# Two blocks of a modulation vector, moved from one attention stage to another

## The chip, the cores and the metric

One core of a Trainium2 chip runs the whole program in one launch. The metric is the device time of that launch in microseconds (us). Three runs of the kernel before were timed, and one more execution was recorded by the hardware profiler.

## The reference, cut to what matters

Two blocks follow each other on 512 tokens of width 1024. The first is a layer with differential attention (4 heads), neighbourhood attention (16 heads), a mixture of 32 experts and a gated per-layer term. The second has two layers, each with its own modulation vector: a grouped-query attention layer, and a latent-attention layer. What matters here is that vector, which depends on the conditions alone and on nothing that the first block computes:

```python
def adaln_params(cond, w_mod, b_mod):
    mod = jax.nn.silu(cond) @ w_mod + b_mod          # w_mod: 1024 x 3072
    return jnp.split(mod, 3, axis=-1)                # shift, scale, gate

def hybrid_layer(x, ctx, c, c_ctx, ...):
    shift, scale, gate = adaln_params(c, w_mod, b_mod)
    h = rms_norm_2(x, norm_w) * (1.0 + scale[:, None, :]) + shift[:, None, :]
    y, yc = mixer(h, hc, mixer_params, cos, sin, with_ctx_out)
    x = x + gate[:, None, :] * y
```

The gate of the second layer is thus first needed when that layer's output is added to x, at the very end of the program. Shift and scale of that layer are needed much earlier, for the context tokens too.

## The kernel before, in words

Everything is in float32, with the large products split in a high and a low part. The stages follow each other: input projections, 4 differential heads and then 4 groups of neighbourhood heads (32 steps in one loop, `run_groups(heads + ...)`, L1341), the output product of that layer, a router, 32 experts whose weights stream in from HBM, a gate, the grouped-query layer (its projections, then 8 pairs of heads of 4 steps each, L1692), its output product, and the latent layer.

**The modulation vectors** come from the generator `mod_steps` (L678). A vector of 3072 columns is computed in 6 blocks of 512 columns. Each block needs 4 transfers of 512 KB (tile `raw`, from the pool RAW), and from each of these 16 small matmuls: 128 x 32 weights (`cv`, the two conditions in a tile that is zero elsewhere) against 128 x 128 of `raw`, one in each quarter of the columns of the array, 64 in a block. DVE adds the bias (`bm`) into `ms` (L707). After 6 blocks `ms` is stored to HBM (L712). Blocks 0 and 1 are the shift, 2 and 3 the scale, 4 and 5 the gate. Four transfers are asked for ahead, one more each time one was used.

**Where its work lies.** `mod_step` (L1333) is called after each of the 32 steps of the loop of L1341 and draws the next block at every second one from step 2: layer 0 at steps 2 to 12, layer 1 at 14 to 24. So all 12 blocks lie beside the differential and neighbourhood heads. The same `mod_step` calls `late` (L1337), which asks for the first four tiles of the output weights `w_out` at step 27, into RAW too, and splits one at each of the steps 29 to 32; at step 30 it asks for the first expert's weights.

**The grouped-query loop.** `gqa_step` (L1688) is called after each of its 32 steps. It draws from `qkv` (projections of later heads, whose weights pass through RAW as well; these end early in the loop) and calls `late` (L1690), which again asks for four tiles of output weights at step 27 and splits them at steps 29 to 32. One step of `attn_pair` (L517 to L530) computes for each of two heads the scores (PE, `s<-stk`), a row maximum (DVE, L524) and the exponentials (ACT, L526) into a tile `pr`, for the second head taken from RAW:

```python
p = ((W, RAW)[h] if nk > 512 else T2)([P, nk], name="pr")
```

The tiles of two steps are transposed together two steps later (`turn_two`, L550), and until then they hold their slots. RAW has 4 slots (`N_RAW`, L36). All loads and stores are issued by one queue, SP, in order (L128). The framework places the instructions on the engines by the order of the program and a simulated time; a tile waits for a free slot of its pool.

Of the kernel before, what the change touches and what calls it, by code (L numbers as in the profile page):

```python
# [17 lines left out]
OP = mybir.AluOpType  # L18
# [4 lines left out]
P = 128  # L23
# [17 lines left out]

PREP_LEAD = 2
D_PRE, GQA_PRE, MLA_PRE = 5, 14, 34
MOD_FROM, EARLY = 2, 30
CTX_FROM, CTX_RATE, CTX_FINE = 2, 1.65, 3
PREL, OVF_AT, PLE_AT, PLE_FIRST = 2, 24, 29, 2
MLA_ST, MLA_FIRST, MLA_MIX = 2, 8, (1, 3)
# [35 lines left out]
def block_kernel(ctx: ExitStack, tc: tile.TileContext, I, out, dbg=None):  # L83
    nc = tc.nc
# [12 lines left out]
    def allocator(p):  # L97
        def f(shape, dt=F32, name=p):
            return pool[p].tile(shape, dt, name=name, tag=p)
        return f  # L100

    XT, RAW, W, Y, K3, T2 = (allocator(p) for p in pool)
# [10 lines left out]
    def D1(dt=F32):  # L113
        return psD.tile([P, 512], dt, name="d1", tag="d1")
# [13 lines left out]
    def load(dst, src):  # L128
        nc.sync.dma_start(dst, src)

    store = load
# [371 lines left out]
    mod_d = [dr.tile([2, 3 * D], F32, name=f"mod{i}") for i in range(2)]  # L503
# [171 lines left out]
        nc.vector.tensor_tensor(y, y, Bs, op=OP.add)  # L675
        return make_X(y, 8)

    def mod_steps(cv):  # L678

        wv = [I[f"l{l}_w_mod_2"].rearrange("(p c) n -> p c n", c=8) for l in range(2)]

        def ask(n):
            t = RAW([P, 2, 512], name="raw")
            load(t, wv[n // 24][:, n % 4 * 2:n % 4 * 2 + 2, n // 4 % 6 * 512:(n // 4 % 6 + 1) * 512])
            return t

        ring = [ask(n) for n in range(4)]
        yield  # L690
        for l in range(2):
            bm = Y([P, 8, P], name="bm")
            nc.vector.memset(bm, 0.0)
            for i in range(2):
                load(bm[i::32], I[f"bm{l}"])
            ms = Y([P, 6, P], name="ms")
            for b in range(6):
                ps = D1()
                for j in range(4):
                    raw = ring.pop(0)  # L700
                    for k in (2 * j, 2 * j + 1):
                        for g in range(4):
                            mm(ps[32 * g:32 * g + 32, :P], cv[:, k], raw[:, k % 2, g * P:(g + 1) * P], k == 0, k == 7)
                    n = 24 * l + 4 * b + j + 4
                    if n < 48:
                        ring.append(ask(n))
                nc.vector.tensor_tensor(ms[:, b], ps[:, :P], bm[:, b], op=OP.add)  # L707
                if b < 5:
                    yield
            nc.vector.scalar_tensor_tensor(ms[:, 2:4], ms[:, 2:4], 1.0, bm[:, 6:8], op0=OP.add, op1=OP.mult)  # L710
            for i in range(2):
                store(mod_d[l][i].rearrange("(b g n) -> g b n", b=6, g=4), ms[i::32])  # L712
            yield

    def rope_rows(name, gains, go, tab, d, scale=1.0):
# [378 lines left out]
    for j, off in enumerate((31, 23, 15)):  # L1094
        load(raw_d[j].rearrange("c h d k -> (h d) c k"), ap_of(I["rpb"], off, [[64, 240], [-1, 16], [1, 32]]))
        t = Y([P, 30, 32], name="btab")
# [102 lines left out]
        pass  # L1199


    cv = T2([P, 8, 32], name="cv")
    c2 = SM([P, 2, 8], "c2", bufs=1)
    cth = SM([P, 2, 8], "cth", bufs=1)
    load(c2, I["c2s"])
    nc.vector.memset(cv, 0.0)
    nc.scalar.activation(cth, c2, AF.Tanh, scale=0.5)
    nc.vector.scalar_tensor_tensor(cth, cth, 1.0, c2, op0=OP.add, op1=OP.mult)
    nc.vector.tensor_scalar(cv[:, :, 0:2], cth.rearrange("p i k -> p k i"), 0.5, None, op0=OP.mult)


    def nbr_group(g):
# [91 lines left out]
        return prep, 4, (A, turn, values), end, LAG_N  # L1304

    beside[0] = False
    fill, units = mod_steps(cv), [0]
    next(fill)
    w_out_v = I["w_out"].rearrange("(c p) n -> p c n", p=P)
    b_out = [Dense(w_out_v, 8, [(b * 512, 512)], OT, place=() if b else [Y] * 6) for b in range(2)]  # L1310
# [236 lines left out]
    _, wts, yidx, oidx, ovf_e, novf = res  # L1547
# [137 lines left out]
    pairs[0] = prepared(pairs[0], qkv, GQA_PRE)  # L1685
    late = split_late(b_out[0], 32)

    def gqa_step():  # L1688
        next(qkv, None)
        late()  # L1690

    run_groups(pairs, gqa_step)  # L1692
    beside[0] = False

    def residual(l, src, bs, fin, nxt=()):

# [118 lines left out]
    todo = list(chain(*grp))  # L1815
# [148 lines left out]
```

## Time and profile before

| what | us |
|---|---|
| three runs of the kernel before, median | 1866.92 |
| lowest and highest of the three | 1862.93, 1869.68 |
| the profiled execution, its device time | 1867.22 |
| span in that profile, first to last instruction | 1865.4 |
| PE busy, share of the span | 1669.5, 89% |
| DVE busy | 968.3, 52% |
| ACT busy | 743.6, 40% |
| POOL busy | 441.3, 24% |

The profile's engines are PE (matmuls), PEld (its weight loads, beside PE), DVE, ACT, POOL and SP (the queue of transfers). The device time is 1.8 us longer than the span. PE is the busiest engine over the whole span, but a share of the span is a mean over stages that have different limits, so each stage is read by itself.

### The profile page before, as it was taken

Reading aid. Unit: us, or ns where it says so; the run is one execution under the profiler, and the core shown is the slowest. Engines: PE = TensorE matmul, PEld = TensorE weight load, DVE = VectorE, ACT = ScalarE, POOL = GpSimd, SP = SyncE. Lnnn points to the kernel's source line nnn. Section 1 sums busy time; section 2 is a strip of 40 time slices with the busy share of each in tenths; the row PEclk is TensorE's granted clock in tenths of the full one; section 3 lists DMA queues with packets and bytes.
Section 4 is the critical chain, followed back from the end, with each engine's and each line's share of the span. In section 5 each row is a group of like instructions: output and inputs, shape, how many; then the busy total and the mean of one; then the engine's idle time right before and its main releaser. Section 6 shows DMA issues by size and latency. Waiting matters only on the chain. (4 is left out here: it accounts for less than half of the span.)

```text
span 1865.4 us, 28201 instructions
## 1 busy us (share of the span) xinstructions
PE 1669.5 (89%) x10297; PEld 1191.7 (64%) x10297; DVE 968.3 (52%) x2237; ACT 743.6 (40%) x1623; POOL 441.3 (24%) x590
## 2 busy tenths in 40 slices
PE   7998878969999989899897799999989889779988
PEld 6887656756555545455553588766657878656757
DVE  6865567343323131311323876666653657886752
ACT  5344557212222222221212443356661534656750
POOL 0531221002221202123101312232111424333221
PEclk9999978979999999999897899999989989999999
DMA  9456667598999999988999452100032435332041
GB/s 253 153 184 221 222 197 226 191 349 312 393 406 402 317 405 335 382 302 307 375 389 376 146 171 90 35 1 1 1 130 96 142 109 165 112 100 63 23 136 46
DMA packets 189983, 385.33 MB, mean 207 GB/s; under 512 B 28184, under 2 KB 86136, under 8 KB 189840
## 3 DMA queue, kind: packets, MB, share of 16 engines
q1 hardware_dynamic: 186384, 375.08, 56.7%
q0 software_dynamic: 3456, 8.39, 1.3%
q8 instruction: 83, 1.36, 0.3%
q14 instruction: 60, 0.49, 0.1%
HBM read 348.86 MB, written 38.13 MB: 207 GB/s over the span
## 5 line engine op out<-in xcount | busy, mean ns | idle before, releaser
L150 PE MATMUL d<-we,exT 128*64 128x256 f32 x2048 | 254.8, 392 | 12.8 <-DMA we<-in_w 8.9
L150 PE MATMUL d<-whi,Xhi 128*128 128x512 f32 (+2 forms) x560 | 219.4, 392 | 3.8 <-ACT Xhi L390 1.5
L150 PE MATMUL d<-whi,Xlo 128*128 128x512 f32 (+2 forms) x560 | 218.1, 390 | 5.2 <-DVE Xlo L182 5.2
L150 PE MATMUL d<-wlo,Xhi 128*128 128x512 f32 (+2 forms) x560 | 217.3, 388 | 0.0
L150 PEld LDWEIGHTS d<-we,exT 128*64 128x64 f32 x2048 | 146.6, 140 | 103.9 <-issue 24.7
L242 ACT CAST whi<-raw 128x1024 fp32r<-128x1024 f32 (+2 forms) x130 | 131.4, 1019 | 134.1 <-PE d L150 80.1
L524 DVE TENSOR_REDUCE ast<-s 128x1 f32<-128x768 f32 (+1 forms) x160 | 135.0, 848 | 77.0 <-PE s L150 75.0
L526 ACT ACTIVATE pr<-s,ast 128x768 f32<-128x768 f32 (+1 forms) x160 | 131.2, 821 | 58.9 <-DVE ast L524 54.6
L153 PE MATMUL t<-ident,pr 128*128 128x128 f32 x832 | 125.8, 280 | 16.4 <-ACT PT L179 9.3
L150 PE MATMUL s<-stk 128*128 128x256 f32 x448 | 121.8, 357 | 20.6 <-ACT pr L526 15.4
L251 DVE TENSOR_TENSOR wlo<-raw,whi 128x1024 fp32r<-128x1024 f32 (+2 forms) x88 | 107.7, 1234 | 40.9 <-ACT whi L242 23.7
L150 PE MATMUL d<-we,eth 128*64 128x512 f32 x512 | 121.8, 608 | 5.3 <-DVE eth L1441 5.3
L150 PEld LDWEIGHTS d<-whi,Xhi 128*128 128x128 f32 x560 | 107.6, 192 | 27.6 <-ACT Xhi L390 3.0
L153 PEld LDWEIGHTS t<-ident,pr 128*128 128x128 f32 x832 | 96.1, 142 | 45.0 <-ACT PT L179 14.2
L248 POOL TENSOR_TENSOR wlo<-raw,whi 128x512 fp32r<-128x512 f32 (+2 forms) x69 | 82.2, 1220 | 178.0 <-ACT whi L242 77.3
L150 PEld LDWEIGHTS d<-whi,Xlo 128*128 128x128 f32 x560 | 107.4, 192 | 26.3 <-DVE Xlo L182 6.7
L150 PE MATMUL d<-whi,ot 128*128 128x512 f32 x384 | 120.1, 392 | 1.9 <-DVE rT L1298 1.3
L150 PEld LDWEIGHTS d<-wlo,Xhi 128*128 128x128 f32 x560 | 107.7, 192 | 19.7 <-DVE wlo L251 0.3
L1433 DVE SCALAR_TENSOR_TENSOR eth<-eth,d 128x256 f32<-128x256 f32 x32 | 13.5, 421 | 156.3 <-ACT eth L1432 152.2
L150 PEld LDWEIGHTS s<-stk 128*128 128x128 f32 x448 | 71.0, 196 | 36.8 <-ACT pr L526 22.5
L150 PEld LDWEIGHTS d<-whi,ot 128*128 128x128 f32 x384 | 71.9, 188 | 19.1 <-issue 1.8
L150 PE MATMUL s<-whi,Xhi 128*128 128x512 f32 (+2 forms) x192 | 75.1, 395 | 9.0 <-ACT pr L526 7.2
(470 smaller groups left out, 3034.3 us busy)
## 6 DMA issues: line engine op xcount, KB each, us to landing
we<-in_w SPq DMA_DIRECT2D x378, 512.0 KB
raw<-in_l_w_mod SPq DMA_DIRECT2D x48, 512.0 KB
raw<-in_l_w_in SPq DMA_DIRECT2D x64, 256.0 KB
raw<-in_w_in SPq DMA_DIRECT2D x24, 512.0 KB
raw<-in_l_w_out SPq DMA_DIRECT2D x24, 512.0 KB
raw<-in_l_w_in SPq DMA_DIRECT2D x16, 512.0 KB
y_d<-ey SPq DMA_DIRECT2D x64, 128.0 KB
bias<-bias SPq DMA_DIRECT2D x48, 128.0 KB
```

The source lines that it names most:

```text
L150: nc.tensor.matmul(o, l, r, start=start, stop=stop)
L153: nc.tensor.transpose(o, x, identr if x.dtype == F32R else ident)
L242: nc.scalar.copy(t, src)
L248: e.tensor_tensor(t, src[:, k], hi[k].bitcast(F32), op=OP.subtract)
L251: e.tensor_tensor(t, src, whole.bitcast(F32), op=OP.subtract)
L524: nc.vector.tensor_reduce(st[:, h:h + 1], ps, op=OP.max, axis=AX.X, negate=True)
L526: nc.scalar.activation(p, ps, AF.Exp, bias=st[:, h:h + 1], accum_out=sums[:, c, h:h + 1])
L1433: nc.vector.scalar_tensor_tensor(th[:, 256:], th[:, :256], 1.0, ps[:, :256], op0=OP.add, op1=OP.mult)
```

## The change

The generator takes a list of parts (layer, first block, last block) and the conditions. In the first loop it is given layer 0 whole and blocks 0 to 3 of layer 1. A second generator with blocks 4 and 5 of layer 1 (the gate) is drawn in `gqa_step` from step 23: at step 23 it makes `cv` again and asks for four transfers, at step 24 it computes block 4, at step 25 block 5 and the stores. Each generator loads its own bias tile.

```diff
--- before.py
+++ after.py
@@ -41,7 +41,7 @@
 
 PREP_LEAD = 2
 D_PRE, GQA_PRE, MLA_PRE = 5, 14, 34
-MOD_FROM, EARLY = 2, 30
+MOD_FROM, EARLY, GATES_FROM = 2, 30, 23
 CTX_FROM, CTX_RATE, CTX_FINE = 2, 1.65, 3
 PREL, OVF_AT, PLE_AT, PLE_FIRST = 2, 24, 29, 2
 MLA_ST, MLA_FIRST, MLA_MIX = 2, 8, (1, 3)
@@ -675,41 +675,48 @@
         nc.vector.tensor_tensor(y, y, Bs, op=OP.add)
         return make_X(y, 8)
 
-    def mod_steps(cv):
+    def mod_steps(cth, parts):
 
 
 
         wv = [I[f"l{l}_w_mod_2"].rearrange("(p c) n -> p c n", c=8) for l in range(2)]
+        todo = [(l, b, j) for l, b0, b1 in parts for b in range(b0, b1) for j in range(4)]
 
         def ask(n):
+            l, b, j = todo[n]
             t = RAW([P, 2, 512], name="raw")
-            load(t, wv[n // 24][:, n % 4 * 2:n % 4 * 2 + 2, n // 4 % 6 * 512:(n // 4 % 6 + 1) * 512])
+            load(t, wv[l][:, j * 2:j * 2 + 2, b * 512:(b + 1) * 512])
             return t
 
-        ring = [ask(n) for n in range(4)]
+        cv = T2([P, 8, 32], name="cv")
+        nc.vector.memset(cv, 0.0)
+        nc.vector.tensor_scalar(cv[:, :, 0:2], cth.rearrange("p i k -> p k i"), 0.5, None, op0=OP.mult)
+        n = 4
+        ring = [ask(i) for i in range(n)]
         yield
-        for l in range(2):
+        for l, b0, b1 in parts:
             bm = Y([P, 8, P], name="bm")
             nc.vector.memset(bm, 0.0)
             for i in range(2):
                 load(bm[i::32], I[f"bm{l}"])
             ms = Y([P, 6, P], name="ms")
-            for b in range(6):
+            for b in range(b0, b1):
                 ps = D1()
                 for j in range(4):
                     raw = ring.pop(0)
                     for k in (2 * j, 2 * j + 1):
                         for g in range(4):
                             mm(ps[32 * g:32 * g + 32, :P], cv[:, k], raw[:, k % 2, g * P:(g + 1) * P], k == 0, k == 7)
-                    n = 24 * l + 4 * b + j + 4
-                    if n < 48:
+                    if n < len(todo):
                         ring.append(ask(n))
+                        n += 1
                 nc.vector.tensor_tensor(ms[:, b], ps[:, :P], bm[:, b], op=OP.add)
-                if b < 5:
+                if b < b1 - 1:
                     yield
-            nc.vector.scalar_tensor_tensor(ms[:, 2:4], ms[:, 2:4], 1.0, bm[:, 6:8], op0=OP.add, op1=OP.mult)
+            if b0 == 0:
+                nc.vector.scalar_tensor_tensor(ms[:, 2:4], ms[:, 2:4], 1.0, bm[:, 6:8], op0=OP.add, op1=OP.mult)
             for i in range(2):
-                store(mod_d[l][i].rearrange("(b g n) -> g b n", b=6, g=4), ms[i::32])
+                store(mod_d[l][i].rearrange("(b g n) -> g b n", b=6, g=4)[:, b0:b1], ms[i::32, b0:b1])
             yield
 
     def rope_rows(name, gains, go, tab, d, scale=1.0):
@@ -1199,14 +1206,11 @@
         pass
 
 
-    cv = T2([P, 8, 32], name="cv")
     c2 = SM([P, 2, 8], "c2", bufs=1)
     cth = SM([P, 2, 8], "cth", bufs=1)
     load(c2, I["c2s"])
-    nc.vector.memset(cv, 0.0)
     nc.scalar.activation(cth, c2, AF.Tanh, scale=0.5)
     nc.vector.scalar_tensor_tensor(cth, cth, 1.0, c2, op0=OP.add, op1=OP.mult)
-    nc.vector.tensor_scalar(cv[:, :, 0:2], cth.rearrange("p i k -> p k i"), 0.5, None, op0=OP.mult)
 
 
     def nbr_group(g):
@@ -1304,7 +1308,7 @@
         return prep, 4, (A, turn, values), end, LAG_N
 
     beside[0] = False
-    fill, units = mod_steps(cv), [0]
+    fill, units = mod_steps(cth, [(0, 0, 6), (1, 0, 4)]), [0]
     next(fill)
     w_out_v = I["w_out"].rearrange("(c p) n -> p c n", p=P)
     b_out = [Dense(w_out_v, 8, [(b * 512, 512)], OT, place=() if b else [Y] * 6) for b in range(2)]
@@ -1685,12 +1689,19 @@
     pairs[0] = prepared(pairs[0], qkv, GQA_PRE)
     late = split_late(b_out[0], 32)
 
+    gates, done = mod_steps(cth, [(1, 4, 6)]), [0]
+
     def gqa_step():
         next(qkv, None)
+        done[0] += 1
+        if done[0] >= GATES_FROM:
+            next(gates, None)
         late()
 
     run_groups(pairs, gqa_step)
     beside[0] = False
+    for _ in gates:
+        pass
 
     def residual(l, src, bs, fin, nxt=()):
```

## Rows read from the trace of the kernel before

**Rows 1.** page, part 2: 40 slices of 46.6 us, in tenths

```profile
PE   7998878969999989899897799999989889779988
PEclk9999978979999999999897899999989989999999
DMA  9456667598999999988999452100032435332041
```

**Rows 2.** windows: length, busy PE, PEld, DVE, ACT, POOL, clock, DMA, GB/s

```profile
250.00:270.00 20.00, 15.54 (x222) 11.26 (x211) 10.68 (x44) 10.28 (x27) 5.52 (x7) 0.83 0.91 282
270.00:290.00 20.00, 16.15 (x184) 11.93 (x185) 14.32 (x51) 13.83 (x37) 4.17 (x7) 0.82 0.71 216
290.00:310.00 20.00, 16.87 (x151) 12.16 (x152) 15.93 (x54) 15.08 (x44) 3.62 (x5) 0.84 0.57 177
```

**Rows 3.** tile cv: matmuls; windows of it (PE, PEld, DVE, clock)

```profile
L150 PE MATMUL d<-raw,cv x768: 269/273/423, 151.5 to 284.5; 128*32 128x128 f32 x192
...
257.00:267.00 10.00, 3.78 (x64) 2.18 (x64) 0.00 (x0) 0.66 1.03 326
280.00:285.00 5.00, 3.61 (x64) 2.76 (x64) 0.00 (x0) 0.72 0.61 214
150.00:290.00 140.00, 34.08 (x768) 22.70 (x768) 0.34 (x2) 0.88 0.71 226
```

**Rows 4.** timeline of PE: start, us, instruction [idle before <- releaser]

```profile
257.95 0.64 PE L150 MATMUL d<-raw,cv 128*32 128x128 f32 x16 [3.09 <-DMA raw<-in_l_w_mod]
...
259.90 1.08 PE L150 MATMUL d<-raw,cv 128*32 128x128 f32 x16 [0.19 <-DMA raw<-in_l_w_mod]
...
262.25 1.08 PE L150 MATMUL d<-raw,cv 128*32 128x128 f32 x16 [0.25 <-DMA raw<-in_l_w_mod]
```

**Rows 5.** tile nsb on ACT, 245 to 285, 285 to 335 us

```profile
L1266 ACT ACTIVATE nsb<-nsb,nst x20: 492/494/512, 252.1 to 282.5; 128x256 f32<-128x256 f32 x20
...
L1266 ACT ACTIVATE nsb<-nsb,nst x36: 488/494/511, 291.4 to 324.3; 128x256 f32<-128x256 f32 x36
```

**Rows 6.** windows of the expert stage, columns as in rows 2

```profile
500.00:600.00 100.00, 92.69 (x630) 55.73 (x630) 30.95 (x98) 24.47 (x66) 17.83 (x24) 1.00 1.03 405
700.00:800.00 100.00, 91.41 (x607) 52.37 (x608) 24.08 (x69) 27.59 (x66) 23.89 (x26) 0.98 0.95 353
```

**Rows 7.** windows of three grouped-query pairs, columns as in rows 2

```profile
1306.30:1326.90 20.60, 18.55 (x118) 12.58 (x117) 13.13 (x21) 13.40 (x27) 3.82 (x4) 1.00 0.00 1
1326.90:1347.60 20.70, 19.37 (x124) 12.99 (x123) 12.77 (x21) 13.77 (x29) 3.71 (x4) 1.00 0.00 1
1347.60:1371.50 23.90, 18.18 (x110) 12.26 (x109) 14.94 (x18) 16.29 (x29) 2.33 (x2) 0.93 0.31 110
```

**Rows 8.** timeline of ACT: first exp of steps 21, 25 and 29

```profile
1326.94 0.90 ACT L526 ACTIVATE pr<-s,ast 128x768 f32<-128x768 f32 x1 [1.17 <-DVE ast L524]
...
1347.63 0.90 ACT L526 ACTIVATE pr<-s,ast 128x768 f32<-128x768 f32 x1 [1.17 <-DVE ast L524]
...
1371.52 0.90 ACT L526 ACTIVATE pr<-s,ast 128x768 f32<-128x768 f32 x1
```

**Rows 9.** timeline of SP's queue; its waits, 1180 to 1400 us

```profile
1352.17 14.09 SPq L129 DMA_DIRECT2D raw<-in_l_w_out  x4
...
1363.44 0.91 SPq L129 DMA_DIRECT2D raw<-in_l_w_out  x2
...
SPq L129 <- PE t L153: 207.4, 4, 171.4
```

**Rows 10.** chain of waits, and PE's timeline, in the same stretch

```profile
1363.98 4.74 DMA raw<-in_l_w_out
...
1370.73 1.65 PE L150 MATMUL s<-stk 128*128 128x256 f32 x4 [3.29 <-ACT pr L526]
```

**Rows 11.** tile bm: count, ns min/median/max, first and last start

```profile
L707 DVE TENSOR_TENSOR ms<-d,bm x12: 273/292/293, 159.1 to 284.9; 128x128 f32<-128x128 f32 x12
L693 DVE MEMSET bm<- x2: 912/912/912, 139.5 to 192.5; 128x1024 f32 x2
```

## The prediction, made before the run

> **What bounds the kernel now.** I read the page's slices first, then the windows of the two stages that the change touches, then single tiles and waits in them. The slices [rows 1] show PE at 7 tenths or more everywhere and no stage in which it rests; DMA is at 8 or 9 tenths in slices 9 to 22 (the experts) and near zero in slices 26 to 28, in which the grouped-query layer lies. So the change takes transfers and matmuls out of a stage with a moderate load on both and puts them where DMA has nothing to do and PE is nearly full.
>
> The stage that loses work: from 250 to 310 us PE is busy for 15.5 to 16.9 of each 20 us, DVE and ACT for 10 to 16, at a granted clock of 0.82 to 0.84 [rows 2]. PE is the busiest, but far from full, and its clock shows it: between the levels of 1.2 and 2.4 GHz it spends a third of the time at the lower. Is the vector's work on the path here? Two readings say mostly yes. PE waited for its transfers, 3.09 + 0.19 + 0.25 = 3.5 us in one block [rows 4], and nothing else can pass in PE's queue meanwhile. And the pace of the neighbourhood groups, read from the exponentials of ACT [rows 5]: 20 of them took 30.4 us while blocks of the vector lay between them, 36 took 32.9 us without. At the later pace, 0.91 us each, 20 take 18.3 us; 12.1 us went elsewhere, and the blocks in that stretch with their waits are about as long.
>
> The stage that gains work: a pair of heads took 20.6 and 20.7 us, with PE busy for 18.55 and 19.37 of that and the clock at 1.00 [rows 7]. PE sets the pace, with 1.3 us free in the second pair. The step of the diff, 23 of 32, lies in that second pair, whose first exponential (step 21) starts at 1326.94 us [rows 8].
>
> **The change part by part.** Taken out beside the neighbourhood heads: 128 of the 768 small matmuls, in the trace those of 257 to 267 and of 280 to 285 us: 3.78 + 3.61 us of PE [rows 3], and the 3.5 us of waits ahead of them [rows 4], 10.9 us in all. If all of it set the pace, 10.9 comes off; the pace reading gives 12.1 as the most. If the other engines took the freed time, no more than the waits would go, 3.5, and nothing excludes less, down to zero, since the framework places the instructions anew. I take PE's own share of the stage without that work, 16.87 of 20 us [rows 2]: 0.84 x 10.9 = 9.2 us. The two additions of DVE (0.29 us each [rows 11]) and eight entries of SP's queue go too; I count nothing, since DVE had a fifth of its time free or more.
>
> Does the gain last? What follows is the output product, the router and the experts, all started later by what this stage takes. In the expert stage PE is busy for 91 to 93 of 100 us and DMA at 0.95 to 1.03 [rows 6], both near full, so it can't absorb a delay and it can't catch up: an earlier start is an earlier end. I keep the 9.2.
>
> Put in beside the grouped-query heads: the same 128 matmuls. At the mean of the stage before, 34.08 us / 768 = 44 ns [rows 3], they are 5.7 us; PE's 1.3 free us of that pair can take a part [rows 7]: 4.4 us. DVE gets a second clearing of the bias tile (0.91 us) besides the two additions and `cv` [rows 11]; it is busy for 13 of 20.7 us, so I count zero, and at most 1.5 if the additions stand in front of a row maximum.
>
> The eight transfers are the unknown. RAW has four slots, and the second head's exponentials need one per step, held until the transposes two steps later. Nothing before shows vector loads here, but the output weights are the same case, one pair later and at the same place in it: four tiles of 512 KB asked for at step 27. The first was issued at 1352.17 and the next at 1363.44 us, when transposes gave slots back; SP stood for 171 us in one wait for these [rows 9]. One then took 4.74 us to land in the chain of waits, and PE stood for 3.29 us behind an exponential that came late [rows 10]. The price of the whole is in the steps: from step 21 to 25 it took 20.69 us, from 25 to 29 23.89 us [rows 8], 3.2 us more, although PE had 1.2 us less to do. That row also holds casts and subtractions that the vector does not need. So four transfers cost between 0 (landed while the pair runs on) and 3.2 us, eight up to 6.4. I take 3.2 for the first four, which meet held slots exactly as those rows do, and half, 1.6, for the others, which are asked for one at a time as small matmuls give slots back.
>
> SP's queue: eight loads, two loads of the bias and two stores stand ahead of the output weights of step 27, and behind those the rows of the modulation and the residual. SP is idle there, so issuing is free; if the last gate load comes late, the output weights do too. One step is 20.69 / 4 = 5.2 us, and I count none of it in the forecast.
>
> The sum, against the profiled execution of 1867.2 us (0.3 above the median of the three runs, 1866.9): 1867.2 - 9.2 + 4.4 + 3.2 + 1.6 = 1867.2. The two sides cancel; I predict **1867 us**.
>
> **A rule weighed.** In the stage before, the clock was 0.66 in the 10 us with the 3.09 us wait [rows 3, 4], and in the pair with the output weights 0.93 where its neighbours had 1.00 [rows 7]. The Trainium skill, in "TensorE: Matmul & The Clock Gate" under "HAM oscillation — how this bites in real kernels", says that short bursts of matmuls with waits for transfers between them drop the clock to half at every wait; it speaks against bringing such bursts into a stage at full clock, and the trace agrees. By that rule both rounds of four would pay the full 3.2 us, and the sum would be 1868.8.
>
> **The rivals.**
>
> Faster: the gate hides. DMA is idle in the stage (0.00 [rows 7]), so the tiles may land within a step, PE has no wait, and only 4.4 us are paid, against the full 10.9 us gained: 1867.2 - 10.9 + 4.4 = 1860.7. For it: no transfer competes. Against: the four slots, and 171 us of SP waiting for them.
>
> Slower: the ring of four takes the slots of `pr`. The late exponential holds back the next scores, both rounds pay 3.2 us, no free time of PE is left for the 5.7 us, and the output weights, behind the gate in the same queue and the same slots, come one step later, 5.2 us: 1867.2 - 9.2 + 5.7 + 6.4 + 5.2 = 1875.3. It decides if the last gate load is issued after about 1352 us of the old time, when the first output weight went out [rows 9].
>
> Slower in another place: the gain ends at the experts, because their transfers keep the same end whenever the stage before is done [rows 6]. Then only the costs stand: 1867.2 + 9.2 = 1876.4. For it: DMA at 1.0. Against: its loads wait for slots that the stage before frees.
>
> That the change does not do what it says: the framework may draw the gate's loads and matmuls ahead of step 23 into gaps of PE. SP's one long wait up to step 27 [rows 9] speaks against much of that; the time would be near that of the faster rival, and its chance is in that one.
>
> **How the numbers follow.** Chances: forecast 0.39, the gate hides 0.33, the ring and the queue 0.18, the gain ends at the experts 0.10. About 0.3%, 5.6 us, is what a measurement of this kernel can tell from no change, so faster means under 1861.3 and slower over 1872.5. The faster rival's middle lies just under its bound: I give 0.28 of its 0.33 to faster and 0.03 of the forecast's, 0.31. Of the two slower ones 0.24 lie above theirs, and 0.03 of the forecast's: 0.27. The rest, 0.42, is no difference. The range runs from 1858 (the faster rival with the 12.1 us of the pace reading, and a little less cost) to 1878 (the slower ones with 1.5 us of DVE).
>
> **What the profile after would show.** Right: 640 small matmuls before 290 us and 128 near 1335 to 1355; the output product starting some 9 us earlier, and the experts by as much; the pair around the gate longer by 6 to 12 us, with waits of PE for a transfer or for a late exponential; the clock there under 1.00. Wrong: the first stage no shorter (other engines had the pace), the earlier start gone by the end of the experts, or the output weights issued a step later than their pair would have it.

## The result, and the profile after

The changed kernel took 1894.2 us (median of 4 runs, 1890.4 to 1900.5), the kernel before 1866.8 us beside it: a ratio of 1.0143, 95% interval 1.0115 to 1.0171. It is 27 us slower, where the prediction had 1867 us and a range up to 1878. Where a loss of a whole kernel is given in us below, it is a ratio's, times 1867 us; a ratio and the quotient of the two medians can differ by 0.2%.

The page of the changed kernel, part 2 (40 slices of 47.5 us, beside [rows 1]):

```profile
PE   7998878969998989898988799889889989879989
PEclk9999978979999989999897799999999989899999
DMA  8447655598999999988898442100133334332031
```

Nothing stands out, so the time has to be found by landmarks: where each stage ends. Five tiles give them in the changed kernel: the first output product (`hx<-d,hx`), the experts (`eth`), the gated product behind them (`pth`), the exponentials of the grouped-query attention (`pr`) and its values matmuls.

```profile
L1377 DVE TENSOR_TENSOR hx<-d,hx x8: 680/690/692, 338.6 to 376.9; 128x512 f32<-128x512 f32 x8
L1436 ACT ACTIVATE eth<-d x32: 369/383/385, 416.6 to 1022.9; 128x256 f32<-128x256 f32 x32
L1621 ACT ACTIVATE pth<-d x8: 582/598/600, 1077.5 to 1123.8; 128x512 f32<-128x512 f32 x8
L526 ACT ACTIVATE pr<-s,ast x64: 895/902/937, 1226.1 to 1424.5; 128x768 f32<-128x768 f32 x64
L150 PE MATMUL d<-PT,gvx x128: 592/592/643, 1269.7 to 1434.6; 128*64 128x512 f32 x128
```

The same tiles in the kernel before:

```profile
L1373 DVE TENSOR_TENSOR hx<-d,hx x8: 681/692/692, 338.6 to 376.9; 128x512 f32<-128x512 f32 x8
L1432 ACT ACTIVATE eth<-d x32: 375/384/386, 416.9 to 1012.8; 128x256 f32<-128x256 f32 x32
L1617 ACT ACTIVATE pth<-d x8: 589/599/602, 1064.6 to 1106.8; 128x512 f32<-128x512 f32 x8
L526 ACT ACTIVATE pr<-s,ast x64: 895/904/948, 1207.2 to 1389.8; 128x768 f32<-128x768 f32 x64
L150 PE MATMUL d<-PT,gvx x128: 592/592/1116, 1247.9 to 1401.4; 128*64 128x512 f32 x128
```

The first output product ends at 376.9 us in both, so the early stage gained nothing. Then the last expert comes 10.1 us later, the gated product another 6.9 us later, and the attention (1207.2 to 1401.4 = 194.2 us before, 1226.1 to 1434.6 = 208.5 us now) takes 14.3 us more. These stages are called A (up to the first output product's last row), B (experts), C (gated product) and E (attention) below. What lies between C and E (100.4 and 102.3 us) and behind E (464.0 and 464.2 us) hardly moves.

**The early stage.** Windows of the changed kernel, columns as in [rows 2], and behind them its small matmuls, as in [rows 3]:

```profile
250.00:270.00 20.00, 15.68 (x164) 11.12 (x164) 13.19 (x51) 10.98 (x29) 6.02 (x8) 0.78 0.81 241
270.00:290.00 20.00, 16.25 (x127) 11.80 (x126) 14.39 (x45) 15.17 (x40) 3.85 (x6) 0.66 0.44 129
```
```profile
L150 PE MATMUL d<-raw,cv x640: 269/273/423, 151.2 to 255.9; 128*32 128x128 f32 x160
```

From 250 to 290 us PE ran 291 matmuls where it ran 406, and was busy for 31.93 us where it was busy for 31.69: the granted clock is at 0.78 and 0.66 where it was at 0.83 and 0.82 [rows 2], nearer to the lower of the two levels. And the waits for transfers [rows 4] made room for waits on the other engines, VectorE above all. One in PE's timeline of the changed kernel:

```profile
257.64 0.65 PE L153 MATMUL t<-ident,rs_y 128*128 128x128 f32 x4 [1.43 <-DVE rs_y L1171]
```

How far the heads had come is read from ACT's exponentials (`nsb`, as in [rows 5]); the table has the first one of some groups of four, in us.

| group | before | after | after is |
|---|---|---|---|
| ahead of the first block that is gone | 252.10 | 253.46 | 1.4 late |
| behind it | 267.35 | 265.42 | 1.9 early |
| the next | 270.42 | 270.65 | 0.2 late |
| ahead of the second block that is gone | 280.99 | 282.57 | 1.6 late |
| behind it | 291.39 | 289.13 | 2.3 early |
| three groups on | 305.40 | 305.15 | 0.3 early |
| later | 313.65 | 313.65 | 0 |

So each block that was gone did bring its heads forward, by 3.3 and 3.8 us, and both times this was lost within some 20 us. Two causes can be read. One is the clock: behind the first block PE was busy for 5.34 of 5.50 us at nearly half clock, and from 300 to 306 us for 5.47 of 6.00 us at half clock, where the kernel before had full clock (the last row here):

```profile
264.00:269.50 5.50, 5.34 (x40) 3.43 (x39) 3.46 (x19) 3.24 (x11) 0.96 (x2) 0.54 0.89 240
300.00:306.00 6.00, 5.47 (x40) 3.87 (x39) 3.51 (x12) 3.20 (x7) 1.75 (x2) 0.50 0.25 67
300.00:306.00 6.00, 4.45 (x48) 3.23 (x48) 4.68 (x16) 4.16 (x10) 1.76 (x2) 1.00 0.16 43
```

The other is VectorE: the exponential at 282.57 us waited 2.14 us for its row, the same one before 0.92 us.

```profile
282.57 0.51 ACT L1270 ACTIVATE nsb<-nsb,nst 128x256 f32<-128x256 f32 x1 [2.14 <-DVE nst L1268]
```
```profile
280.99 0.51 ACT L1266 ACTIVATE nsb<-nsb,nst 128x256 f32<-128x256 f32 x1 [0.92 <-DVE nst L1264]
```

**The attention.** Windows of two pairs in the changed kernel (columns as in [rows 7]); their bounds are the first exponentials of steps 21, 25 and 29 (as in [rows 8]):

```profile
1348.67:1370.78 22.11, 19.45 (x145) 12.47 (x143) 12.19 (x18) 13.38 (x28) 3.71 (x4) 1.00 0.22 67
1370.78:1405.23 34.45, 26.02 (x215) 17.03 (x216) 15.34 (x21) 15.95 (x29) 2.31 (x2) 0.86 0.45 151
```

The pair in which the gate begins lost 1.4 us (22.11 against 20.70 [rows 7]), the next one 10.6 us (34.45 against 23.90): 12.0 of the stage's 14.3 us. Over both, PE was busy for 45.5 us where it was busy for 37.6, and idle for 11.1 where it was idle for 7.0. SyncE's queue in the changed kernel (as in [rows 9]), then its longest waits of 1200 to 1420 us and PE's timeline:

```profile
1353.19 28.36 SPq L129 DMA_DIRECT2D raw<-in_l_w_mod  x8
...
1393.27 6.80 SPq L129 DMA_DIRECT2D raw<-in_l_w_out  x4
```
```profile
SPq L129 <- PE t L153: 144.1, 4, 117.2
...
SPq L129 <- PE d L150: 15.8, 4, 9.6
```
```profile
1365.57 0.64 PE L150 MATMUL d<-raw,cv 128*32 128x128 f32 x16
1370.07 0.64 PE L150 MATMUL d<-raw,cv 128*32 128x128 f32 x16 [1.02 <-DMA raw<-in_l_w_mod]
1372.82 1.08 PE L150 MATMUL d<-raw,cv 128*32 128x128 f32 x16 [2.11 <-DMA raw<-in_l_w_mod]
...
1390.96 0.65 PE L150 MATMUL d<-raw,cv 128*32 128x128 f32 x16
```

The eight tiles were issued over 28 us: SyncE waited for RAW slots that an exponential's transposes (PE t; its 117.2 us lie ahead of the first tile) or the gate's own matmuls (PE d) had to let go. The matmuls so came in eight groups over 26 us, and the output weights stood behind all of it: at 1393.27 us, 22.5 us behind step 25, where it had been 4.5 us (1352.17 and 1347.63 [rows 8, 9]). PE's waits for the gate's transfers come to 4.2 us between steps 21 and 29, those for late exponentials to 4.6 us, no more than before (5.7 us):

```profile
PE s L150 <- ACT pr L526: 4.6, 4, 2.7
PE d L150 <- DMA raw<-in_l_w_mod: 4.2, 3, 2.1
```

The rest of the loss lies 130 us ahead of the gate: from the first exponential of step 1 to that of step 5 the stage took 37.5 us where it took 34.5 (the kernel before is the first row; the 166 matmuls are as many):

```profile
1207.20:1241.73 34.53, 32.06 (x166) 25.97 (x164) 21.13 (x52) 14.76 (x36) 9.03 (x22) 1.00 0.00 1
1226.06:1263.52 37.46, 33.72 (x166) 27.03 (x164) 21.88 (x53) 14.48 (x36) 9.91 (x22) 0.95 0.01 2
```

The framework placed one instruction of the gate on VectorE there, the clearing of its bias tile, and the row maximum behind it came 0.9 us later than before, the exponential behind that 2.4 us, and PE was at a lower clock for a while:

```profile
1233.77 0.91 DVE L699 MEMSET bm<- 128x1024 f32 x1 [0.16 <-issue]
```

**The experts.** Late in this stage two rows of the second layer's modulation (tile `mrow`) are loaded for the context path. From 800 to 1000 us the instructions of that tile waited for the two transfers 8.9 us in the changed kernel, and 0.5 us in the kernel before (one line of each):

```profile
  DMA mrow<-mod: 8.9, 2
```
```profile
  DMA mrow<-mod: 0.5, 1
```

In the changed kernel PE's part of it and SyncE's queue ahead of it read so:

```profile
901.79 7.19 PE L150 MATMUL t<-mrow,ones_row 1*128 1x512 f32 x8 [4.20 <-DMA mrow<-mod]
```
```profile
885.50 0.65 SPq L129 DMA_DIRECT2D raw<-in_l_w_kv_b  x1
...
888.06 0.58 SPq L129 DMA_DIRECT2D raw<-in_l_w_kv_b  x1
...
891.90 0.55 SPq L129 DMA_DIRECT2D raw<-in_l_w_kv_b  x1
...
895.83 1.49 SPq L129 DMA_DIRECT2D mrow<-mod  x2
```

`mrow` stands behind three weight tiles; in the kernel before it stands behind one:

```profile
885.18 0.65 SPq L129 DMA_DIRECT2D raw<-in_l_w_kv_b  x1
...
889.02 0.25 SPq L129 DMA_DIRECT2D mrow<-mod  x1
```

No line of the experts was edited. The windows of B and C, in the kernel before and in the changed one (columns as in [rows 2]):

```profile
376.94:1012.81 635.87, 567.59 (x3662) 337.02 (x3661) 185.41 (x536) 145.83 (x346) 115.72 (x125) 0.94 0.96 362
1012.81:1106.77 93.96, 81.07 (x330) 58.85 (x331) 66.60 (x135) 43.33 (x83) 18.52 (x18) 0.89 0.48 164
```
```profile
376.91:1022.91 646.00, 574.67 (x3662) 342.93 (x3661) 185.74 (x536) 145.20 (x345) 116.65 (x125) 0.93 0.95 357
1022.91:1123.83 100.92, 86.92 (x330) 62.47 (x331) 67.04 (x135) 44.06 (x83) 16.81 (x18) 0.85 0.44 151
```

The same matmuls kept PE busy for 7.1 us more in B and 5.9 us more in C, at a granted clock of 0.93 for 0.94 and 0.85 for 0.89. So of the 17.0 us lost in the two stages 13 show up as slower matmuls, and 4 as idle time. Three things were to be settled: why the attention paid 14 us and not 9, where B and C come from, and why A gave nothing.

### The profile page after: what moved, and what is told of

Read it like the earlier page. It is cut to its first block, busy times and chain, and to the rows that moved or that the text cites. A ratio compares the mean times of both kernels' runs of the same rounds, so it can differ in the third digit from the quotient of the medians.

```text
span 1898.8 us, 28203 instructions
## 1 busy us (share of the span) xinstructions
PE 1695.3 (89%) x10297; PEld 1207.7 (64%) x10297; DVE 969.7 (51%) x2240; ACT 743.1 (39%) x1623; POOL 440.0 (23%) x590
## 5 line engine op out<-in xcount | busy, mean ns | idle before, releaser
L150 PE MATMUL d<-we,exT 128*64 128x256 f32 x2048 | 255.9, 395 | 11.5 <-DMA we<-in_w 8.5
L150 PEld LDWEIGHTS d<-we,exT 128*64 128x64 f32 x2048 | 149.2, 141 | 102.3 <-issue 25.2
```

Of the source, the lines that this page charges most:

```text
L150: nc.tensor.matmul(o, l, r, start=start, stop=stop)
```

## The experiments

All times are medians beside the kernel before on the same chip (1866.6 to 1868.1 us in all series). Stages are in us from one trace each; "mrow" is the wait for its transfers as above. The kernel before is the first row, the changed kernel the second. "12 @2" means twelve early blocks that begin at step 2 of the neighbourhood heads.

| kernel | early | late gate | median | ratio [95%] | A | B | mrow | C | E |
|---|---|---|---|---|---|---|---|---|---|
| before | 12 @2 | - | 1866.8 | 1 | 376.9 | 635.9 | 0.5 | 94.0 | 194.2 |
| after | 10 @2 | RAW | 1894.2 | 1.0143 [1.0115, 1.0171] | 376.9 | 646.0 | 8.9 | 100.9 | 208.5 |
| e1 | 10 @2 | RAW | 1891.5 | 1.0132 [1.0090, 1.0174] | 375.2 | 640.9 | 8.9 | 100.3 | 207.6 |
| e2 | 12 @2, new code | - | 1871.5 | 1.0026 [1.0001, 1.0052] | 375.4 | 640.1 | 3.1 | 94.6 | 193.2 |
| e3 | 10 @2 | none | 1882.2 | 1.0066 [1.0038, 1.0094] | 377.1 | 646.8 | 11.6 | 102.7 | 194.2 |
| e4 | 12 @2 | RAW, again | 1883.1 | 1.0088 [1.0057, 1.0118] | 372.7 | 634.8 | 0 | 91.8 | 209.2 |
| e5 | 10 @2 | pool Y | 1881.2 | 1.0070 [1.0046, 1.0093] | 376.6 | 641.3 | 9.5 | 101.7 | 193.8 |
| e6 | 12 @2 | matmuls alone | 1872.6 | 1.0018 [0.9995, 1.0042] | 377.1 | 640.1 | 0 | 93.2 | 198.5 |
| e7 | 12 @2 | transfers alone | 1872.9 | 1.0031 [1.0015, 1.0046] | 373.9 | 635.8 | 0.4 | 93.8 | 197.8 |
| e8 | 10 @6 | none | 1872.7 | 1.0027 [1.0010, 1.0044] | 372.8 | 647.3 | 11.4 | 92.7 | 195.7 |
| e9 | 12 @4 | - | 1883.2 | 1.0099 [1.0067, 1.0130] | 375.8 | 640.4 | 7.9 | 97.2 | 193.6 |
| e10 | 10 @3 | pool Y | 1870.3 | 1.0014 [0.9995, 1.0033] | 372.2 | 637.9 | 0.2 | 94.5 | 197.5 |
| e11 | 10 @3 | none | 1865.4 | 0.9994 [0.9977, 1.0012] | 370.3 | 636.9 | 0.6 | 95.4 | 194.9 |
| e12 | 10 @3 | RAW | 1883.0 | 1.0093 [1.0065, 1.0121] | 370.7 | 637.9 | 1.0 | 94.4 | 209.3 |
| e13 | 12 @3 | - | 1872.2 | 1.0013 [0.9996, 1.0030] | 373.6 | 645.1 | 5.2 | 95.1 | 193.9 |
| e14 | 10 @4 | pool Y | 1873.8 | 1.0031 [1.0013, 1.0048] | 374.5 | 640.1 | 1.4 | 96.9 | 196.5 |

The medians of one kernel's series and its one trace differ by some us (the traces of the changed kernel, e3 and e6 are the slowest of their series, those of e4, e9 and e12 the fastest), so a stage is read from several kernels that share it.

### e1: the changed kernel again

> The changed kernel once more, with a second profile. Theory 'added': in the first profile the eight steps that hold the gate and the output weights (steps 21 to 29 of the grouped-query loop) take 56.6 us, 12 us longer than before, and that stands in every execution. Theory 'order': the experts end 13 us later than before although they start at the same time, because the framework queued their transfers in another order; then this too stands in every execution. Rival 'chance': the 13 us in the experts belong to that one execution (it was 6 us above the median of its four runs); then this profile shows the experts ending within 7 us of the kernel before. Time by all: 1890 to 1898.

1891.5 us, and the same stages but for 5 us in B. The last expert came 3.3 us behind that of the kernel before (1016.1 and 1012.8 us), within the 7 us that were the sign of the rival, chance: about half of the first trace's 10 us in B was that one execution's. The other half came again, and so did C and E.

### e2: the gate back in the early stage, with the new code

```diff
-    fill, units = mod_steps(cth, [(0, 0, 6), (1, 0, 4)]), [0]
+    fill, units = mod_steps(cth, [(0, 0, 6), (1, 0, 4), (1, 4, 6)]), [0]
...
-            next(gates, None)
```

> The new generator, but the gate again as a third part beside the neighbourhood heads; nothing beside the grouped-query heads. Theory 'added': the 12 us there are gone, and the first stage is as it was: 1866 to 1872. Theory 'order': the early part is as full as before, so the experts' transfers come in the old order: 1866 to 1872 too. Rival 'form': the new generator itself (its second bias tile, its own small tile of conditions) costs: near 1890.

1871.5 us. The new generator as such costs at most half a per cent.

### e3: no gate for the second layer

```diff
+                if b1 == 4:
+                    store(mod_d[l][i].rearrange("(b g n) -> g b n", b=6, g=4)[:, 4:6], ms[i::32, 0:2])
...
-            next(gates, None)
```

> The gate's two blocks are left out altogether; the shift's values are stored in their place. Nothing is added beside the grouped-query heads, and the first stage has the lighter load of the changed kernel. By my prediction's step, 9 us gained: 1858. Theory 'added' with no gain in the first stage (the first profile has that stage ending at the same time): 1867, and the whole loss of the change lies in the grouped-query stage. Theory 'order': the lighter first stage alone makes the experts longer: 1875 to 1883.

1882.2 us: with 128 matmuls and eight transfers left out altogether, the kernel is slower than before (12 us by the ratio), by B and C. E is back at 194.2 us.

### e4: the gate in both places

```diff
-    fill, units = mod_steps(cth, [(0, 0, 6), (1, 0, 4)]), [0]
+    fill, units = mod_steps(cth, [(0, 0, 6), (1, 0, 6)]), [0]
```

> All twelve blocks beside the neighbourhood heads as before, and the gate a second time beside the grouped-query heads. Theory 'added': 12 us over the kernel before, 1879, more if the early parts of that loop suffer too (1884); the experts end as before. Theory 'order': as much only if nothing upstream moves; the 13 us of the experts are absent, as the first stage is full again. If this takes 1890 or more, the addition alone makes the whole loss and the experts' 13 us come from it too.

E is 209.2 us, and A, B and C are no longer than before. So the loss is two losses: that of the attention (e4, 16 us) and one ahead of it (e3, 12 us); with their intervals they make up the 27 us.

### e5 to e7: slots, matmuls or transfers

e5 takes the late gate's tiles from another pool, Y, which has 14 slots:

```diff
+    def mod_steps(cth, parts, ring_of=RAW):
-            t = RAW([P, 2, 512], name="raw")
+            t = ring_of([P, 2, 512], name="raw")
...
+    gates, done = mod_steps(cth, [(1, 4, 6)], Y), [0]
```

> The changed kernel, with the late gate's eight [128, 2, 512] tiles taken from pool Y instead of RAW, where the grouped-query attention's own weights and the output product's early weights also lie. From the stage's first exp-tile to its last values matmul the attention took 194.2 us before and 208.5 and 207.6 us in two traces of the changed kernel. Theory A, the slots: the gate's tiles hold RAW slots that the output weights wait for and back up SP's queue; with slots of their own the stage falls to 194 to 200 us, and the kernel gains 8 to 14 us on the changed one (1878 to 1886 us beside about 1892). Theory B, the matmuls: 128 small products among the attention's make TensorE wait for DMAs and set back the exps whatever the slots; the stage stays at 204 to 210 us and the kernel within 4 us of the changed one. Theory C, both: 200 to 204 us.

E falls to 193.8 us, as if there were no gate. The gate's transfers (first and last issue), then its matmuls on PE's timeline, then the output weights on SyncE's queue:

```profile
L129 SPq DMA_DIRECT2D raw<-in_l_w_mod x8: 367/390/1105, 1189.4 to 1315.1; - x8
```
```profile
1357.28 1.07 PE L150 MATMUL d<-raw,cv 128*32 128x128 f32 x28
...
1362.66 1.51 PE L150 MATMUL d<-raw,cv 128*32 128x128 f32 x46
```
```profile
1369.87 12.07 SPq L129 DMA_DIRECT2D raw<-in_l_w_out  x4
```

The last tile was issued 42 us ahead, the 128 matmuls ran in 6.9 us with no wait for a transfer, and the output weights went out 7.8 us behind step 25 (1362.08) and not 22.5. Two things differ from the changed kernel at once, the slots and the early loading that they allow; no run parts them.

e6 and e7 add one half each to the kernel with all blocks early. e6 takes the matmuls on a tile already in SBUF:

```diff
+            if still is not None:
+                return still
...
+    gates, done = mod_steps(cth, [(1, 4, 6)], vx.rearrange("p c n -> p (c n)").rearrange("p (a n) -> p a n", a=2)), [0]
```

> All twelve gate blocks beside the neighbourhood heads as before, and in the grouped-query attention the gate's two blocks once more as matmuls alone: 128 products on a tile that lies in SBUF from earlier, with no weight transfers and no store (what is left out: the second gate's transfers and its result). With the transfers the same arrangement took 209.2 us for the attention stage, against 194.2 without any gate there. Theory A, the slots and transfers cost it: the stage falls to 194 to 198 us, and the kernel is at 1867 to 1872 us. Theory B, TensorE's work costs it: the stage is 203 to 210 us and the kernel at 1877 to 1884 us. From the prediction's own term (128 matmuls at 44.4 ns, less the free time): 198 to 200 us.

e7 takes the transfers, with a copy of one column on POOL that lets each go:

```diff
+                    if touch:
+                        nc.gpsimd.tensor_copy(ms[:, b, j:j + 1], raw[:, 0, 0:1])
-                    for k in (2 * j, 2 * j + 1):
+                    for k in (2 * j, 2 * j + 1) if not touch else ():
```

> All twelve gate blocks beside the neighbourhood heads as before, and in the grouped-query attention the gate's eight weight tiles once more as transfers alone, through the RAW slots, each let go by a copy of one column on POOL (what is left out: the second gate's matmuls and store). Theory A, the slots and transfers: the attention stage is 203 to 210 us as with the whole gate, and the kernel at 1877 to 1884 us. Theory B, TensorE's work: 194 to 198 us and 1867 to 1872 us.

E without a gate is 194.2 us (mean of the seven traces, 193.2 to 195.7). The matmuls alone make it 198.5 (+4.3), the transfers alone 197.8 (+3.6). In e7 SyncE's queue shows the slots at work, with the output weights 11.7 us behind step 25 (1349.69):

```profile
1333.34 22.59 SPq L129 DMA_DIRECT2D raw<-in_l_w_mod  x8
...
1361.39 7.66 SPq L129 DMA_DIRECT2D raw<-in_l_w_out  x4
```

Neither theory holds alone, and the two numbers must not be added. Between the first exponentials of steps 1, 5, 21 and 29 and the end of the stage lie, in us:

| kernels | 1 to 5 | 5 to 21 | 21 to 29 | 29 to the end |
|---|---|---|---|---|
| no late gate (seven traces) | 34.5 | 85.1 to 86.4 | 44.1 to 45.3 | 28.4 to 30.0 |
| e6, matmuls alone | 37.4 | 85.2 | 45.6 | 30.2 |
| e7, transfers alone | 37.5 | 85.2 | 45.7 | 29.5 |
| both through RAW (four traces) | 36.0 to 37.5 | 85.2 to 86.8 | 53.3 to 56.6 | 29.4 to 31.9 |
| both in pool Y (e5, e10, e14) | 35.4 | 84.4 to 86.0 | 45.4 to 45.5 | 28.4 to 31.1 |

Most of what e6 and e7 added, 2.9 us in each, lies in steps 1 to 5, where each has the clearing of the bias tile and neither has anything else of the gate on an engine: it is one cost, met twice. Beside the gate (steps 21 to 29, 44.5 us in the mean without it) the matmuls alone cost 1.1 us, the transfers alone 1.2, both through RAW 10.9 (mean of four), both in pool Y 1.0. So some 8.6 us come only when the two meet in the ring. In e6 the matmuls ran where PE had been idle, at full clock (3.1 us idle of 45.6, where it was 7.0 of 44.6 in the kernel before); in the changed kernel 11.1 us were idle, and the clock was lower:

```profile
1335.46:1357.14 21.68, 20.78 (x191) 13.76 (x190) 12.80 (x21) 13.35 (x28) 4.75 (x5) 1.00 0.00 1
1357.14:1381.07 23.93, 21.75 (x174) 14.96 (x172) 16.02 (x22) 16.18 (x29) 2.33 (x2) 1.00 0.28 93
```

How they meet is argued from the waits above and not shown by a run of its own: a matmul waits for its tile, the tile's slot stays taken until the matmul has run, and the next tile and the output weights wait for that slot. Over the whole stage the gate costs 14.4 us through RAW (208.7, mean of four) and 1.7 us in pool Y (193.8, 197.5 and 196.5).

### e8: no gate, blocks begun later

```diff
-MOD_FROM, EARLY, GATES_FROM = 2, 30, 23
+MOD_FROM, EARLY, GATES_FROM = 6, 30, 23
```

> The kernel without the second layer's gate anywhere (the gate's two blocks are left out and the shift's values stored in their place), as in the run without the gate, but the ten blocks that are left begin four steps later, so that the last one stands where the twelfth stood before. That earlier run took 1882.2 us, 15.6 us more than the kernel before, of it some 11 us between the first output product and the last expert and 9 us between there and the end of the gate stage behind the experts. Theory A, the load: work taken away from the neighbourhood heads does harm wherever the blocks stand; again 1878 to 1886 us. Theory B, the order: what harmed is that transfers of later stages were queued in another order once the blocks ended earlier; with the last block in its old place most of the loss is gone, 1864 to 1872 us. Between them, 1872 to 1878 us, neither is shown.

1872.7 us, between the windows. Stage C is back (92.7 us), B is not (647.3): the same work in another order is 7 us faster than e3, and the loss ahead of the attention is two things, in B and in C.

What "order" means here: the framework that builds the program lays out each engine's instructions, and code far from an edit can come out in another sequence. Read from the traces: ahead of the first `mrow` in the experts SyncE's queue has one weight tile in the kernel before and in e2, e4, e6 and e7, and three in the changed kernel, e3, e5 and e8, and PE's sequence in the experts differs between the two groups as well. The three-tile order also comes out of the kernel before, with nothing moved or left out, when its blocks begin at 4. That gives the next runs.

### e9: the kernel before, begun two steps later

```diff
-MOD_FROM, EARLY = 2, 30
+MOD_FROM, EARLY = 4, 30
```

> The kernel before with one constant changed: its twelve gate blocks begin two steps of the neighbourhood heads later (4 instead of 2). Nothing is left out, added or moved to another stage. SyncE's queue as it was built then has, in the experts, the order that the changed kernel has (two input-weight loads ahead of the context loads, where the kernel before has them behind), and that the kernel before does not have. Theory A, the order: the stage from the first output product to the last expert takes 641 to 648 us as in the four kernels built that way (five traces, 640.9 to 647.3), against 635 to 640 in the five traces with the old order, and the kernel is at 1872 to 1882 us. Theory B, the two blocks' absence does it: 635 to 640 us there, and the kernel at 1864 to 1869 us.

1883.2 us: one constant, no work moved between stages, and the kernel is 1.0% slower. The wait of the experts comes with it (7.9 us). C is 97.2 us. The kernel's time lies just over theory A's window and B, at 640.4 us, just under it, in a trace that is the fastest of its series.

### e10 to e12: the order of before, with ten blocks

Begun at 3, the ten blocks leave SyncE's queue in the experts in the order of before.

```diff
-MOD_FROM, EARLY, GATES_FROM = 2, 30, 23
+MOD_FROM, EARLY, GATES_FROM = 3, 30, 23
```

e10 is e5 with it, e11 is e3 with it, e12 the changed kernel with it.

> The changed kernel with the late gate's tiles in pool Y, as in the run with slots of its own (1881.2 us), and the ten early blocks beginning one step later (3 instead of 2), with which SyncE's queue in the experts comes out in the order of the kernel before. Theory A, order and slots are all of the loss: the experts take 635 to 640 us, the stages behind them 92 to 96 us, the attention 194 us, and the kernel 1862 to 1871 us. Theory B, the work that left the early stage matters by itself: 1878 to 1884 us as with the old start.

> The kernel without the second layer's gate anywhere (the gate's two blocks are left out and the shift's values stored in their place), its ten blocks beginning one step later (3 instead of 2), with which SyncE's queue in the experts comes out in the order of the kernel before. Begun at 2 it took 1882.2 us and begun at 6, with the same order in the experts as at 2, 1872.7. Theory A, the order: the loss in the experts goes as well, 1862 to 1870 us. Theory B, less work beside the neighbourhood heads does harm: 1873 to 1884 us.

> The changed kernel (its late gate through RAW), with the ten early blocks beginning one step later (3 instead of 2), with which SyncE's queue in the experts comes out in the order of the kernel before. Theory A, two separate losses: the experts and what follows them are back at 635 to 640 and 92 to 96 us, the attention stage still takes 205 to 210 us, and the kernel is at 1877 to 1884 us, half of the loss gone. Theory B, one loss: still 1888 to 1896 us.

1870.3, 1865.4 and 1883.0 us: by the ratios 10, 13 and 7 to 9 us off the same kernels begun at 2, all three as theory A had it. B is 636.9 to 637.9 us, C 94.4 to 95.4, and e12 keeps the attention's loss. A is 4 to 7 us shorter in them as well, which no theory had.

e10 is the changed kernel with both losses mended, and it is level with the kernel before: its A is 4.7 us shorter, its B 2.0 and its E 3.3 us longer. e11 has no gate at all, and it is level too (0.9977 to 1.0012): not even a gate that costs nothing would have brought more than 0.23% in this order.

### e13 and e14: is it the start or the number of blocks?

e13 is the kernel before with 3, e14 is e10 with 4.

```diff
-MOD_FROM, EARLY = 2, 30
+MOD_FROM, EARLY = 3, 30
...
-MOD_FROM, EARLY, GATES_FROM = 3, 30, 23
+MOD_FROM, EARLY, GATES_FROM = 4, 30, 23
```

> The kernel before with one constant changed: its twelve gate blocks begin one step of the neighbourhood heads later (3 instead of 2); nothing is left out. The three kernels with ten blocks that begin at 3 ended the first output product at 370.3 to 372.2 us, the ones with ten blocks that begin at 2 at 375.2 to 377.1, as with twelve (372.7 to 377.1). Theory A, two blocks less do shorten that stage by some 5 us, and begun at 2 another order takes it back: here it ends at 374 to 377 us and the kernel is at 1864 to 1870 us. Theory B, the start alone gives the 5 us: it ends at 369 to 373 us, the kernel at 1859 to 1864 us, and the two blocks are worth nothing there.

> The changed kernel with the late gate's tiles in pool Y and the ten early blocks beginning at step 4 (2 in the changed kernel, 3 in the run at 1870.3 us); the queue orders in the experts and behind them come out as with 3. Theory A, two blocks less shorten the early stage wherever they begin, but for the start at 2: the first output product ends at 369 to 373 us and the kernel is at 1862 to 1871 us. Theory B, it was the start at 3: it ends at 374 to 377 us and the kernel is at 1869 to 1876 us.

A is 373.6 us with twelve blocks at 3, between the two windows, and 374.5 with ten at 4, as theory B had it. Side by side by start, twelve and ten blocks: at 2, 375.2 (mean of five, 372.7 to 377.1) and 376.5 (mean of four); at 3, 373.6 and 371.1 (mean of three); at 4, 375.8 and 374.5. So part of the 5 us was the start; the two blocks are worth -1 to +2.5 us of A, which is less than the 4.4 us by which the five traces with twelve blocks at 2 differ. And e13 spoils too simple a story of B: it has the one-tile order, though not quite PE's sequence of before, yet `mrow` waits 5.2 us, B is 645.1 us, and the kernel is slower than either theory had it.

## Why the prediction was wrong

**The early gain, "0.84 x 10.9 = 9.2".** Failed. It was 0 in the changed kernel, and -1 to +2.5 us by start in the runs. The sum took what a block frees as time off the stage, at an unchanged clock. Each block did bring its heads forward (3.3 and 3.8 us), but the stage did not keep it: with 115 matmuls fewer from 250 to 290 us PE's clock was lower and its busy time equal, so that the heads behind a gap ran slower on a nearly full PE, and PE and ACT waited for VectorE's rows. The bound that was named for this ("nothing excludes less, down to zero") was the case; the clock of 0.82 to 0.84 [rows 2] was read as a sign of free time, and that it would fall with the work was in no term. How much of the loss is the clock's and how much VectorE's was not separated by a run.

**"The expert stage can't absorb a delay, and it can't catch up."** Failed, and it is the largest miss. The prediction took the stages between as unchanged since no line of them was. They lost 17 and 11 us in two traces of the changed kernel (10.1 + 6.9, and 5.0 + 6.3 in e1). Removing two blocks changed the order in which the framework laid out the instructions of later stages; e9 shows that such an order costs as much with all work in place, and e10 to e12 that most of the loss goes when the order does. In B the mark of it is the late `mrow`: with three tiles ahead of it (six traces) it waits 7.9 to 11.6 us and B is 640.4 to 647.3 us, with one (ten traces) 0 to 5.2 us and, but for e13, 634.8 to 640.1. The two groups touch at 640, and their means, 643.8 and 638.5, are as far apart as two traces of the changed kernel (646.0 and 640.9), so this is a mark and not a measure. In C it is VectorE's sequence, as read from the traces: where it is that of before (before, e4, e6, e7) C is 91.8 to 94.0 us, where it is that of the changed kernel (after, e1, e3, e5, e9) 97.2 to 102.7, and in three other sequences 92.7 to 96.9. The granted clock goes with it: 0.85 to 0.87 in C in the changed kernel, e1, e3 and e5, 0.88 to 0.91 in all others, e9 among them. None of the rivals was this. Which instruction of C's sequence does it, whether the lower clock is its cause or its effect, and what else decides B (e13), stays open.

**The attention, "4.4 + 3.2 + 1.6 = 9.2".** The ring was named, but every term was off. Beside the gate the matmuls alone cost 1.1 us and not 4.4, the transfers alone 1.2 and not 4.8, and both through the same four slots 10.9: the sum had no term for their meeting. That the whole stage in e6 was 4.3 us longer, next to 4.4 and inside the 198 to 200 us expected from that term, is luck, since 2.9 of it lie in steps 1 to 5. These 2.9 us go with the clearing of the bias tile, for which the sum counted zero, "and at most 1.5 if the additions stand in front of a row maximum"; it was the clearing that stood there, and in another place. The slower rival (5.7 + 6.4 + 5.2 = 17.3 us) had the ring and the late output weights, with its deciding point: the last gate tile issued after about 1352 us of the old time. It came at 1381.55 us, less 21.7 us that step 21 was late, 1359.8. It was the better forecast for this stage and had a chance of 0.18, though it too added up the parts one by one.

**The rule weighed.** From 1370.78 us, with eight short groups of matmuls and waits between, the granted clock was 0.86 where it had been 0.93 [rows 7]; in e10, with the same matmuls on tiles loaded ahead, the window of the gate is at full clock:

```profile
1344.00:1370.00 26.00, 24.74 (x255) 17.16 (x254) 16.85 (x23) 17.15 (x32) 2.33 (x2) 1.00 0.15 48
```

The Trainium skill, in "TensorE: Matmul & The Clock Gate" under "HAM oscillation — how this bites in real kernels", says that bursts parted by waits for transfers lose the clock; these rows agree. By that rule the sum came to 1868.8 us, so it named the danger and not its size.

**The signs.** Of those that were given for right, 640 small matmuls early (they ended at 255.9 us), a longer pair with waits for transfers (12.0 us over the two pairs) and a clock under 1.00 came; late exponentials came too, but no more than before, and an earlier output product did not. Two of the signs given for wrong came: the first stage no shorter, and the output weights more than a step late (22.5 us behind step 25, 4.5 before).

## What to carry to other kernels

Before costing work that moves between stages, ask which ring of slots its tiles will use there and who else waits for that ring: here the same gate cost 14.4 us in a shared ring of four and 1.7 us in a larger pool, loaded ahead. Time that is freed on an engine counts only if it is still there at the end of the stage: follow one landmark through the stage, and look at the granted clock behind the gap, since here 3.3 and 3.8 us were won and lost again within 20 us each. When two halves of a change are run alone, read where in the stage each one's cost lies before adding them: here one cost far ahead was in both. Where a framework lays out the instructions, run the kernel before with one harmless constant shifted: here a shift by two steps alone moved the time by 1.0%, as much as the parts of the change that one wanted to explain, and a shift by one step by 0.1%.

## What was not expected of the hardware

Less work on TensorE took as much busy time: from 270 to 290 us 184 matmuls needed 16.15 us at a clock of 0.82 [rows 2], and 127 needed 16.25 us at 0.66. The counts differ in the small products, but the same ones became slower too: four transposes took 1.11 us at 265.50 us in the changed kernel and 0.66 us at 267.26 us in the kernel before. And 128 products that took 6.9 us on tiles loaded ahead (e5) spread over 26 us where their tiles came one by one.
